# Convolution mixer of a four-layer trunk: TensorE's order written by hand, last shifted inputs copied between partitions, other priorities

## The chip, the cores and the metric

The kernel runs on one core of a Trainium2 chip. Five engines work side by side, each through its own list of instructions in order: TensorE (matmul, with its weight loads), VectorE (DVE), ScalarE (ACT), GpSimd (POOL) and SyncE (SP), whose queue issues the DMA copies. TensorE has a clock with two levels, 2.4 GHz and 1.2 GHz; the profile shows the level that was granted as a share of the full one. The metric is the device time of one execution in microseconds (us); less is better.

## The reference

A trunk of four layers over 512 tokens of 1024 channels, batch 1, float32. Each layer has a token mixer and a gated feed-forward block; each is framed by a modulation from a conditioning vector and a layer norm. The mixer of layer 0 is the one that the change touches:

```python
def conformer_conv_module(h, w_pw1, b_pw1, dw_w, dw_b, ln_g, ln_b, w_pw2, b_pw2):
    u = jax.nn.glu(h @ w_pw1 + b_pw1, axis=-1)          # 1024 -> 2 x 1024, a * sigmoid(g)
    u = causal_dwconv(u, dw_w, dw_b)                    # 31 taps along the tokens, per channel
    u = jax.nn.silu(layer_norm(u, ln_g, ln_b))          # norm over the 1024 channels
    return u @ w_pw2 + b_pw2

# around each mixer and each feed-forward block f
h = x * (1.0 + scale) + shift                           # shift, scale, gate: silu(c) @ ada_w + ada_b
x = layer_norm(DN_ALPHA * x + (1.0 + gate) * f(h), post_ln_g, post_ln_b)
```

## The kernel before

**Arithmetic.** A matrix product in float32 is made of three products of a cheaper type: weights and activations are each split into a high and a low part (hi and lo), and hi x hi, hi x lo and lo x hi are summed in PSUM. One block of weights (128 x 1024) is a unit: a 512 KB load by SP into `raw` (r_...), a ScalarE copy (wh_..., L282) and a VectorE subtraction (wl_..., L284), in units of the gated second projections preceded by a product with the gate row (L272). For the first projection a unit of 128 output channels is then 24 matmuls (L312).

**Layer 0's mixer** (`conformer`) runs over j = 0 to 7, blocks of 128 channels. Each takes two units of the first projection, one for the value (pa) and one for the gate (pg). ScalarE makes the sigmoid sg (L703), VectorE multiplies (L706) into `upad`, which has 30 zeros in front. The 31 taps are shared: the first three are VectorE operations on `upad` (L724, L726), the other 28 are matmuls. For these, R holds the input four times, shifted by 0 to 3 tokens and regrouped so that 32 channels x 4 shifts fill the 128 partitions: `upad` is written to DRAM (ud, L709) and read back by four copies (L711). lw (L714) are the diagonal weights. The convolution of block j (c0 to c7 in the text, `pc` in the trace, L720) is 28 matmuls, each shown as two. VectorE adds the two parts (cv, L728), TensorE transposes the sum to token-major form (ct, L692), ScalarE copies it (tm, L694), VectorE takes the statistics (L696). R and lw have two buffers each; the first projection has four PSUM banks, pc two, and the transposes and the gate's products share two (tr).

**Beside it** run the ada units: 48 per layer, each a load of 512 KB and a VectorE reduction (L238). `fill` adds one behind each unit of the projection (16 in this stage); `flush` brings those of a range that are still missing. Units 16 to 23 give the mixer's gate, 24 to 39 the modulation of the feed-forward block that follows. The gate is spread to a row by eight dg pieces (L472), two products on TensorE (gb, L475) and two ScalarE copies (L476).

**The end of the mixer.** For each 128 tokens t, `rstd` (L648 to L651, the power on POOL) and `normalise` (one half on VectorE, L660, one on ScalarE, L663) make the norm. For each half s of the tokens (two t's) and each j, TensorE transposes back (cb, L745), ScalarE applies silu (cs, L747), and ScalarE and VectorE split the result (cuh, cul). The second projection (p_pw with wh_pw first, L381) has eight units, whose 192 matmuls begin with the first three units on the first half of the tokens. Its results are added to X (L624), normalised and turned to the next h (hl, hh), with which the feed-forward block starts (p_f).

**What sets the order.** The program is traced in the order of the code; a scheduler then lists each engine's instructions by a simulated time and by priority, which is the place in the code unless `high_priority(offset)` moves it ahead by that many places (weights: 150). Where `manual_schedule` names an engine, that engine keeps the order of the code. The order of each list is fixed at compile time; at run time each engine takes its list in order and waits on semaphores.

Of the kernel before, what the change touches and what calls it, by code (L numbers as in the profile page):

```python
# [160 lines left out]
class Trunk:  # L161
# [504 lines left out]
    def conformer(self, nxt):  # L666
# [9 lines left out]
        with self.pool(name="cf", bufs=1, reuse_waits="tile") as op, ExitStack() as es, \  # L676
# [21 lines left out]
            self.apool, self.abufs = cf, CB  # L698
            for j in range(KD):
                pa = self.up(ins["pw1"], j, "pw1", fills=1)  # L700
                pg = self.up(ins["pw1"], KD + j, "pw1", fills=1)
                sg = self.sp.tile([P, T], F32, tag="u", bufs=4, name=f"sg{j}")
                nc.scalar.activation(out=sg, in_=pg, func=AF.Sigmoid, bias=bp1(KD + j))  # L703
                u = cf.tile([P, 544], F32, tag="upad", bufs=2, name=f"upad{j}")
                nc.vector.memset(u[:, :pad], 0.0)
                nc.vector.scalar_tensor_tensor(out=u[:, pad:pad + T], in0=pa, scalar=bp1(j), in1=sg, op0=ALU.add, op1=ALU.mult)  # L706
                R = cf.tile([P, 4, 544], F32, tag="R", bufs=2, name=f"R{j}")
                ud = dr.tile([P, 544], F32, tag="ud", bufs=2, name=f"ud{j}")
                nc.sync.dma_start(out=ud[:, nd:pad + T], in_=u[:, nd:pad + T])  # L709
                for q in range(4):  # L710
                    nc.sync.dma_start(out=R[32 * q:32 * q + 32, :, nd:pad + T - q],  # L711
                                      in_=ud[:, nd + q:pad + T].rearrange("(b c) x -> c b x", c=32))
                lw = cf.tile([P, CONV_G * 4, 32], F32, tag="lw", bufs=2, name=f"lw{j}")
                nc.vector.tensor_tensor(out=lw, in0=m4.rearrange("p (a c) -> p a c", a=1).broadcast_to([P, CONV_G * 4, 32]),  # L714
                                        in1=wpe[:, j, :].rearrange("p (a c) -> p a c", c=1).broadcast_to([P, CONV_G * 4, 32]),
                                        op=ALU.mult)
                pc = self.bank(f"pc{j}", "pc")
# [5 lines left out]
                o = cv[j]  # L723
                nc.vector.tensor_scalar(out=o, in0=u[:, :T], scalar1=dww(0, j), scalar2=dwb(j), op0=ALU.mult, op1=ALU.add)  # L724
                for tap in range(1, nd):
                    nc.vector.scalar_tensor_tensor(out=o, in0=u[:, tap:tap + T], scalar=dww(tap, j), in1=o,  # L726
                                                   op0=ALU.mult, op1=ALU.add)
                nc.vector.tensor_tensor(out=o, in0=pc, in1=o, op=ALU.add)  # L728
                token_major(j)
            self.flush(i, 24)  # L730
            self.apool = None
            gate = self.gate_rows(op, i, 0)
            es.close()
# [3 lines left out]
            for s in range(2):  # L737
                for t in (2 * s, 2 * s + 1):
                    mv = self.rstd(st[t], f"cf{t}")
                    self.normalise(tm[:, t, :], tm[:, t, :], mv)  # L740
                hs = slice(2 * s * P, 2 * (s + 1) * P)
# [686 lines left out]
```

## Time and profile before

| | us |
|---|---|
| median of 3 runs | 2688.15 |
| lowest and highest | 2685.92, 2689.37 |
| profiled execution | 2686.62 |
| its span, first to last instruction | 2684.8 |
| TensorE busy | 2603.4 |
| VectorE busy | 1992.3 |
| ScalarE busy | 1193.2 |

The profile is of one execution. Its times count from the first instruction; 1.82 us of the execution lie outside the span. The mixer of layer 0 takes about the first 240 us. A busy time of TensorE is the sum of matmul records, which overlap while they stream: a row of many matmuls that starts every 0.23 us is TensorE at its peak. The text in brackets behind a row of the timeline is the idle time of the engine just before it and what ended it.

### The profile page before, as it was taken

The numbers are of one execution on the slowest core, as the hardware profiler recorded it, in microseconds if no ns is written. First come the engines' busy times: TensorE is split into PE (matmuls) and PEld (weight loads), VectorE is DVE, ScalarE is ACT, GpSimd is POOL, SyncE is SP. The second block draws the span as 40 slices with busy tenths as digits, with TensorE's granted clock in tenths as the row PEclk, the third lists the DMA queues.
The fourth block names the chain that finished last, engine by engine and source line by source line (L and its number), as shares of the span: only waits on it lengthen the run. The fifth ranks groups of instructions, "written<-read, shape, count | busy, mean of one in ns | idle before, by whom it ended". The sixth has DMA issues, their size and how long they took to land.

```text
span 2684.8 us, 33858 instructions
## 1 busy us (share of the span) xinstructions
PE 2603.4 (97%) x13044; PEld 2095.9 (78%) x13044; DVE 1992.3 (74%) x3068; ACT 1193.2 (44%) x1758; POOL 43.8 (2%) x80
## 2 busy tenths in 40 slices
PE   8989999999997999999999999999999999999998
PEld 6548888887876788888887778888887777888886
DVE  7579997775778799677766777998676576766676
ACT  3134433345874543434545544543434454543432
POOL 0000000000000000000000000000000000000000
PEclk9989999999998999999999999999999999999999
DMA  8754864233221486222322223774323211323222
GB/s 320 211 170 162 302 231 142 98 102 102 85 66 45 155 303 204 98 97 95 100 81 71 95 81 108 244 256 158 100 97 94 94 56 48 102 98 115 94 96 77
DMA packets 109529, 352.66 MB, mean 131 GB/s; under 512 B 12088, under 2 KB 22328, under 8 KB 109368
## 3 DMA queue, kind: packets, MB, share of 16 engines
q1 hardware_dynamic: 109368, 350.50, 39.3%
q8 instruction: 102, 1.67, 0.3%
q14 instruction: 59, 0.48, 0.1%
HBM read 341.96 MB, written 8.50 MB: 131 GB/s over the span
## 4 chain that ended last, share of the span: by engine, by line
PE 83%; DVE 8%; ACT 5%; DMA 2%; issue 2%; POOL 1%; SPq 0%; POOLq 0%; DVEq 0%; ACTq 0%
PE p_f L312 35%; PE p_d L381 16%; PE p_mup L312 6%; PE p_mdn L381 3%; PE p_pw L312 3%; PE p_hqf L312 2%; PE p_sqk L312 2%; PE pc L720 1%; PE p_hv L381 1%; PE p_sv L381 1%; PE p_hg L312 1%; PE ms L1029 1%; ACT hf L545 1%; PE tr L540 1%; PE mn L1168 1%
## 5 line engine op out<-in xcount | busy, mean ns | idle before, releaser
L312 PE MATMUL p_f<-hl,wh_f 128*128 128x512 f32 (+1 forms) x1504 | 565.3, 376 | 1.9 <-DVE hl L552 1.9
L312 PE MATMUL p_f<-hh,wl_f 128*128 128x512 f32 (+1 forms) x1504 | 564.8, 376 | 0.0
L312 PE MATMUL p_f<-hh,wh_f 128*128 128x512 f32 (+1 forms) x1504 | 564.0, 376 | 0.1
L282 ACT CAST wh_f<-r_f 128x1024 fp32r<-128x1024 f32 x176 | 185.1, 1053 | 337.8 <-PE p_f L312 309.6
L312 PEld LDWEIGHTS p_f<-hl,wh_f 128*128 128x128 f32 x1504 | 283.1, 188 | 53.7 <-DVE hl L552 2.5
L312 PEld LDWEIGHTS p_f<-hh,wh_f 128*128 128x128 f32 x1504 | 282.5, 188 | 52.6 <-ACT hh L551 1.4
L312 PEld LDWEIGHTS p_f<-hh,wl_f 128*128 128x128 f32 x1504 | 283.1, 188 | 51.2 <-issue 0.2
L284 DVE TENSOR_TENSOR wl_f<-r_f,wh_f 128x1024 fp32r<-128x1024 f32 x176 | 215.2, 1224 | 134.3 <-ACT wh_f L282 133.8
L238 DVE CUSTOM_DVE_ANT_0 ada<-ada,sbc,adab 128x1024 f32<-128x1024 f32 x192 | 244.0, 1281 | 3.4 <-DMA ada<-in_ada_dram 3.4
L1359 DVE SCALAR_TENSOR_TENSOR cv<-p_f,par,cv 128x511 f32<-128x511 f32 (+1 forms) x176 | 131.5, 747 | 1.4
L1359 DVE SCALAR_TENSOR_TENSOR cg<-p_f,par,cg 128x511 f32<-128x511 f32 (+1 forms) x176 | 131.5, 747 | 1.3
L272 DVE TENSOR_TENSOR r_d<-r_d,gate 128x1024 f32<-128x1024 f32 x88 | 107.5, 1222 | 30.4 <-DMA r_d<-in_fdn_dram 29.9
L1369 ACT ACTIVATE cg<-cg 128x512 f32<-128x512 f32 x88 | 55.3, 629 | 159.3 <-DVE cg L1359 159.3
L284 DVE TENSOR_TENSOR wl_d<-r_d,wh_d 128x1024 fp32r<-128x1024 f32 x88 | 107.5, 1221 | 9.8 <-ACT wh_d L282 9.7
L312 PE MATMUL p_mup<-hh,wh_mup 128*128 128x512 f32 (+1 forms) x280 | 107.3, 383 | 0.9 <-ACT hf L545 0.9
L312 PE MATMUL p_mup<-hh,wl_mup 128*128 128x512 f32 (+1 forms) x280 | 106.1, 379 | 0.0
L312 PE MATMUL p_mup<-hl,wh_mup 128*128 128x512 f32 (+1 forms) x280 | 105.5, 377 | 0.0
L282 ACT CAST wh_d<-r_d 128x1024 fp32r<-128x1024 f32 x88 | 92.2, 1048 | 19.9 <-PE p_f L312 15.6
L663 ACT ACTIVATE X<-X,mv 128x512 f32<-128x512 f32 x56 | 43.1, 810 | 78.0 <-DVE mv L651 78.0
L1357 ACT ACTIVATE cg<-p_f,par 128x512 f32<-128x512 f32 x88 | 68.1, 774 | 13.9 <-PE p_f L312 13.9
L381 PE MATMUL p_d<-wl_d,gr2h 128*128 128x512 f32 x176 | 68.8, 391 | 0.0
L381 PE MATMUL p_d<-wl_d,gr0h 128*128 128x512 f32 x176 | 68.8, 391 | 0.0
(473 smaller groups left out, 5614.6 us busy)
## 6 DMA issues: line engine op xcount, KB each, us to landing
ada<-in_ada_dram SPq DMA_DIRECT2D x192, 512.0 KB, 4.6
r_f<-in_fup_dram SPq DMA_DIRECT2D x176, 512.0 KB, 4.0
r_d<-in_fdn_dram SPq DMA_DIRECT2D x88, 512.0 KB, 3.3
r_mup<-in_mup_dram SPq DMA_DIRECT2D x32, 512.0 KB, 3.3
r_pw<-in_pw_dram SPq DMA_DIRECT2D x24, 512.0 KB, 7.5
r_hqf<-in_hqf_dram SPq DMA_DIRECT2D x16, 512.0 KB, 3.3
r_mdn<-in_mdn_dram SPq DMA_DIRECT2D x16, 512.0 KB, 3.3
r_sqk<-in_sqk_dram SPq DMA_DIRECT2D x16, 512.0 KB, 3.5
```

Of the source, the lines that this page charges most:

```text
L238: nc.vector.tensor_tensor_reduce(out=raw, in0=raw, in1=self.sbc, scale=1.0, scalar=ab[:, j:j + 1], op0=ALU.mult, op1=ALU.add, accum_out=ac ...
L272: nc.vector.tensor_tensor(out=r, in0=r, in1=gr, op=ALU.mult)
L282: nc.scalar.copy(hi, raw)
L284: nc.vector.tensor_tensor(out=lo, in0=raw, in1=hi.bitcast(F32), op=ALU.subtract)
L312: self.nc.tensor.matmul(ps[:, c0:c1], a, b[:, k, c0:c1], start=(n == 0), stop=(n == 3 * KD - 1))
L381: self.nc.tensor.matmul(bank, l[:, ts_], r, start=(kp == first and a == n == 0), stop=(kp == last and a == 1 and n == 2))
L540: nc.tensor.transpose(ps[:, j * P:(j + 1) * P], n[:, k * P:(k + 1) * P], self.ident)
L545: nc.scalar.activation(out=hf[:, j, :], in_=ps[:, j * P:(j + 1) * P], func=AF.Identity, scale=G[:, k:k + 1], bias=B[:, k:k + 1])
L663: nc.scalar.activation(out=o[:, hs], in_=x[:, hs], func=AF.Identity, scale=mv[:, 2:3], bias=mv[:, 3:4])
L1357: nc.scalar.activation(out=o, in_=ps, func=AF.Identity, scale=w[2], bias=par[:, C_CONVB + m:C_CONVB + m + 1])
L1359: nc.vector.scalar_tensor_tensor(out=o[:, s:], in0=ps[:, :T - s], scalar=w[2 - s], in1=o[:, s:], op0=ALU.mult, op1=ALU.add)
L1369: nc.scalar.activation(out=cg, in_=cg, func=AF.Silu)
```

## The change

The change stays inside `conformer`. (1) The loop over j is cut into pieces, `unit`, `gating`, `convolve`, `back` and `gates`, which are put into one list, sorted by a number, and traced under `manual_schedule` for TensorE. The order that results on TensorE is: units 0 to 6, c0, u7, ct0, c1, u8, ct1, c2, u9, ct2, u10, c3, u11, ct3, u12, c4, u13, ct4, u14, c5, u15, ct5, the two gate products, c6, ct6, c7, ct7 (u: unit of the first projection, value and gate of a block in turn). (2) For the last block, j = 7, the write to DRAM and the four copies back are replaced by sixteen copies straight from `upad` to R, 32 partitions each. (3) Gating and lw get a priority of 200, the sum with its transposes, copy and statistics 400, and `rstd` and `normalise` 400. (4) Only units 0 to 12 bring an ada fill. (5) Behind the eighth sigmoid the table of silu is loaded ahead.

```diff
+            def unit(n):
+                j, z = divmod(n, 2)
+                px[n] = self.up(ins["pw1"], z * KD + j, "pw1", fills=int(n < 13))
+                if z:
+                    with tc.high_priority(offset=SPRIO):
+                        gating(j)
+            def gating(j):
                 sg = self.sp.tile([P, T], F32, tag="u", bufs=4, name=f"sg{j}")
+                act = nc.scalar.activation(out=sg, in_=px[2 * j + 1], func=AF.Sigmoid, bias=bp1(KD + j))
+                if j == KD - 1:
+                    with tc.issue_after(act.ins):
+                        nc.scalar.preload_act_table_set("silu_and_others")
...
+                if j == KD - 1:
+                    for q in range(4):
+                        for b in range(4):
+                            nc.sync.dma_start(out=R[32 * q:32 * q + 32, b, nd:pad + T - q], in_=u[32 * b:32 * b + 32, nd + q:pad + T])
+                else:
+                    ud = dr.tile([P, 544], F32, tag="ud", bufs=2, name=f"ud{j}")
...
+            def convolve(j):
+                R = us["R", j]
+                with tc.high_priority(offset=SPRIO):
+                    lw = cf.tile([P, CONV_G * 4, 32], F32, tag="lw", bufs=2, name=f"lw{j}")
...
+            def back(j):
+                with tc.high_priority(offset=2 * SPRIO):
+                    nc.vector.tensor_tensor(out=cv[j], in0=pcs[j], in1=cv[j], op=ALU.add)
+                    token_major(j)
+
+            def gates():
+                self.flush(i, 24)
+                us["gate"] = self.gate_rows(op, i, 0)
+
+            todo = [(n, lambda n=n: unit(n)) for n in range(2 * KD)] + [(2 * KD - 0.5, gates)]
+            for j in range(KD):
+                todo.append((min(max(2 * j + 4.5, j + 6.5), 2 * KD + 0.2 * (j - KD)), lambda j=j: convolve(j)))
+                todo.append((min(max(2 * j + 5.6, j + 7.4), 2 * KD + 0.2 * (j - KD) + (0.1 if j > 5 else -0.05)), lambda j=j: back(j)))
+            todo.sort(key=lambda x: x[0])
+            with tc.manual_schedule(engines={mybir.EngineType.PE}):
+                for _, fn in todo:
+                    fn()
...
                 for t in (2 * s, 2 * s + 1):
-                    mv = self.rstd(st[t], f"cf{t}")
-                    self.normalise(tm[:, t, :], tm[:, t, :], mv)
+                    with tc.high_priority(offset=2 * SPRIO):
+                        mv = self.rstd(st[t], f"cf{t}")
+                        self.normalise(tm[:, t, :], tm[:, t, :], mv)
```

## Rows read from the trace of the kernel before

**Rows 1.** The page, part 1: busy us (share of the span) and instructions of each engine.

```profile
PE 2603.4 (97%) x13044; PEld 2095.9 (78%) x13044; DVE 1992.3 (74%) x3068; ACT 1193.2 (44%) x1758; POOL 43.8 (2%) x80
```

**Rows 2.** Table of stretches: length, then busy us (instructions) by engine, granted clock, DMA share, GB/s.

```profile
155.80:175.90 20.10, 16.31 (x124) 4.71 (x122) 11.04 (x20) 3.85 (x5) 0.00 (x0) 0.92 0.41 102
175.90:189.10 13.20, 5.12 (x18) 2.45 (x15) 9.78 (x26) 6.29 (x10) 3.31 (x4) 0.62 0.80 287
189.10:200.20 11.10, 11.10 (x55) 8.74 (x54) 10.51 (x28) 9.58 (x21) 0.00 (x0) 0.84 0.49 162
200.20:221.00 20.80, 20.80 (x93) 17.22 (x92) 20.45 (x27) 7.36 (x9) 0.00 (x0) 1.00 0.44 142
```

**Rows 3.** Timeline, TensorE's matmuls: start us, us, engine, line, what, times [idle before <-releaser].

```profile
49.09 0.50 PE L312 MATMUL p_pw<-hh_first,wh_pw 128*128 128x512 f32 x1
49.43 0.40 PE L312 MATMUL p_pw<-hl_first,wh_pw 128*128 128x512 f32 x1
49.66 0.40 PE L312 MATMUL p_pw<-hh_first,wl_pw 128*128 128x512 f32 x1
...
95.85 0.66 PE L692 MATMUL ct<-ident,cv 128*128 128x128 f32 x4 [0.81 <-DVE cv L728]
...
158.01 0.72 PE L692 MATMUL ct<-ident,cv 128*128 128x128 f32 x4 [2.20 <-DVE cv L728]
...
167.38 0.63 PE L692 MATMUL ct<-ident,cv 128*128 128x128 f32 x4 [0.92 <-DVE cv L728]
...
169.73 6.22 PE L720 MATMUL pc<-R,lw 128*32 128x512 f32 x56
...
180.47 1.12 PE L692 MATMUL ct<-ident,cv 128*128 128x128 f32 x4 [4.52 <-DVE cv L728]
...
182.26 2.07 PE L475 MATMUL gb<-dg,onesr 128*128 128x512 f32 x2 [0.67 <-ACT tm L694]
...
185.60 1.09 PE L745 MATMUL cb<-ident,tm 128*128 128x128 f32 x4 [1.26 <-DVE tm L660]
...
189.10 1.20 PE L381 MATMUL p_pw<-wh_pw,cuh 128*128 128x512 f32 x2
...
240.81 0.39 PE L312 MATMUL p_f<-hl,wh_f 128*128 128x256 f32 x1 [0.72 <-DVE hl L552]
```

**Rows 4.** Timeline of VectorE, the same columns.

```profile
49.08 1.61 DVE L706 SCALAR_TENSOR_TENSOR upad<-p_pw,cpar,sg 128x512 f32<-128x512 f32 x2 [0.32 <-ACT sg L703]
...
153.65 1.28 DVE L238 CUSTOM_DVE_ANT_0 ada<-ada,sbc,adab 128x1024 f32<-128x1024 f32 x1
...
170.46 2.36 DVE L272 TENSOR_TENSOR r_pw<-r_pw,gate 128x1024 f32<-128x1024 f32 x2 [0.93 <-ACT gate L476]
...
179.73 0.69 DVE L728 TENSOR_TENSOR cv<-pc,cv 128x512 f32<-128x512 f32 x1
...
187.77 1.22 DVE L272 TENSOR_TENSOR r_pw<-r_pw,gate 128x1024 f32<-128x1024 f32 x1
```

**Rows 5.** The chain of waits in order of time: start us, us, what.

```profile
158.73 7.78 PE pc L720 x56
...
208.51 1.22 DVE wl_pw L284
```

**Rows 6.** Timeline of SP's queue: issue start us, us, what, number of copies.

```profile
58.33 2.83 SPq L711 DMA_DIRECT2D R<-ud  x4
...
155.87 1.75 SPq L711 DMA_DIRECT2D R<-ud  x4
```

**Rows 7.** DMA issues of 140 to 185 us: queue, number, KB, median us to landing.

```profile
ud<-upad SPq DMA_DIRECT2D x1, 269.5 KB, 2.5
...
R<-ud SPq DMA_DIRECT2D x1, 268.0 KB, 6.0
```

**Rows 8.** Timeline of ScalarE, columns as in rows 3.

```profile
186.39 1.28 ACT L747 ACT_TABLE_LOAD   x1
...
187.69 0.56 ACT L747 ACTIVATE cs<-cb,cpar 128x256 f32<-128x256 f32 x1
```

More of the change, by code (lines that the diff above doesn't have):

```diff
@@ new lines, in conformer @@
+            us, pcs, px = {}, {}, {}
+            def unit(n):
[5 more added lines that the diff above has]
+            def gating(j):
+                sg = self.sp.tile([P, T], F32, tag="u", bufs=4, name=f"sg{j}")
+                act = nc.scalar.activation(out=sg, in_=px[2 * j + 1], func=AF.Sigmoid, bias=bp1(KD + j))
+                if j == KD - 1:
+                    with tc.issue_after(act.ins):
+                        nc.scalar.preload_act_table_set("silu_and_others")
+                u = us[j] = cf.tile([P, 544], F32, tag="upad", bufs=2, name=f"upad{j}")
+                nc.vector.memset(u[:, :pad], 0.0)
+                nc.vector.scalar_tensor_tensor(out=u[:, pad:pad + T], in0=px[2 * j], scalar=bp1(j), in1=sg, op0=ALU.add, op1=ALU.mult)
+                R = us["R", j] = cf.tile([P, 4, 544], F32, tag="R", bufs=2, name=f"R{j}")
+                if j == KD - 1:
[4 more added lines that the diff above has]
+                    ud = dr.tile([P, 544], F32, tag="ud", bufs=2, name=f"ud{j}")
+                    nc.sync.dma_start(out=ud[:, nd:pad + T], in_=u[:, nd:pad + T])
+                    for q in range(4):
+                        nc.sync.dma_start(out=R[32 * q:32 * q + 32, :, nd:pad + T - q],
+                                          in_=ud[:, nd + q:pad + T].rearrange("(b c) x -> c b x", c=32))
+                o = cv[j]
+                nc.vector.tensor_scalar(out=o, in0=u[:, :T], scalar1=dww(0, j), scalar2=dwb(j), op0=ALU.mult, op1=ALU.add)
+                for tap in range(1, nd):
+                    nc.vector.scalar_tensor_tensor(out=o, in0=u[:, tap:tap + T], scalar=dww(tap, j), in1=o,
+                                                   op0=ALU.mult, op1=ALU.add)
@@ new lines, in convolve @@
+            def convolve(j):
+                R = us["R", j]
+                with tc.high_priority(offset=SPRIO):
+                    lw = cf.tile([P, CONV_G * 4, 32], F32, tag="lw", bufs=2, name=f"lw{j}")
+                    nc.vector.tensor_tensor(out=lw, in0=m4.rearrange("p (a c) -> p a c", a=1).broadcast_to([P, CONV_G * 4, 32]),
+                                            in1=wpe[:, j, :].rearrange("p (a c) -> p a c", c=1).broadcast_to([P, CONV_G * 4, 32]),
+                                            op=ALU.mult)
+                pc = pcs[j] = self.bank(f"pc{j}", "pc")
@@ L722, in conformer @@
                                          tile_position=(0, 32 * cb))
[L723 to L730, printed above, removed]
+            def back(j):
[13 more added lines that the diff above has]
+                    fn()
             self.apool = None
-            gate = self.gate_rows(op, i, 0)
+            gate = us["gate"]
             es.close()
```

17 lines of the change are left out of this document (removed).

## Prediction

> **What bounds the kernel now.** I read the page first: TensorE is busy 97% of the span [rows 1], so whatever the change gives must come from a stretch where TensorE stands still or runs at half clock. The table of stretches of the convolution mixer, read next, shows where that is: while units and convolutions mix, TensorE is full; from 155.8 to 175.9 us it is busy 16.3 of 20.1 us, and from 175.9 to 189.1 us only 5.1 of 13.2 us, at a granted clock of 0.62 on the mean, between the half level (1.2 GHz) and the full one (2.4 GHz) [rows 2]. Third the timeline of TensorE there: it waits 2.20 us for the sum cv5, 0.9 us for cv6, 4.52 us for cv7 and 1.26 us for the first normalised tile, and starts the second projection (p_pw with wh_pw, L381) at 189.10 [rows 3]. Fourth the timeline of VectorE: those sums are late since it works in order and other work stands ahead of them, three ada reductions in front of cv5, and weights of the second projection (L272, L284) in front of cv7 [rows 4]. Last the chain of waits: through the second projection it runs over VectorE (from 208.5 us on) and comes back to TensorE at the start of the feed-forward block, which waits 0.72 us for hl before 240.81 [rows 3, 5]. VectorE is busy 10.5 of 11.1 and 20.5 of 20.8 us there [rows 2]. So two limits lie close together: TensorE up to 189 us, VectorE just behind it after.
>
> Call E the moment at which all sixteen units, c0 to c5 (the convolutions) and ct0 to ct4 (their transposes) are done. Before, E is 158.01 - 2.20 = 155.81 us and the second projection starts 33.3 us later. Except for the 3.8 us of ada work below, the engines' total work is unchanged; what changes is the order.
>
> **The change, part by part.**
>
> *Order by hand up to E.* The sum of TensorE's work is the same; c5 moves ahead of the last unit, which alone gains nothing. Two known waits change. The wait of ct1 at 95.85 (0.81 us) goes, because a unit now stands between c1 and ct1: -0.8. Unit 4 now comes strictly before unit 5 and takes the PSUM bank that the first upad operation reads until about 49.08 + 0.75 = 49.83 us, where TensorE before started another unit at 49.09 [rows 3, 4]: +0.7. New is that c0 stands behind unit 6 and holds back everything after it until R0 has landed. It is due at 49.83 + 3 units x 24 matmuls x 0.23 us = 66.4 us [rows 3]. R0 was issued from 58.33 to 61.2 us [rows 6] and the slowest of these copies in the late stretch landed 6.0 us after its issue [rows 7]: 67.2 us. So 0 to 0.8 us; I take 0, since the new priority puts upad's copy ahead of the ada loads. E stays at 155.7 us.
>
> *From E to c7.* Now ct5 (0.4 us), two gate products (2.07 us for one at half clock [rows 3], so 1.0 to 1.1 each), c6, ct6, c7. The second gate product needs ct5's bank back (a ScalarE copy, behind the last sigmoid and perhaps the table load) and four dg pieces on VectorE behind upad7 and three taps: c6 starts between E + 2.6 (no wait) and E + 5.7; I take 4.3. c6 lasts 6.2 us; the sum, now first in VectorE's queue, and ct6 take 0.74 us to ct's start [rows 3, 4] and some 0.9 more for drain and ct: c7 could start at E + 12.1.
>
> *R7 directly.* A write to DRAM (landing in 2.5 us) and four copies go; sixteen small copies come. All sixteen are issued by SP one after another: four took 1.75 us [rows 6], so 0.44 us each and 7.0 us in all, where one write and four copies cost 2.2 us of issue. Sigmoid and upad end about E + 1.6, the last issue begins at E + 8.3, and landing takes 2.5 (the write alone) to 6.0 us (the last of four big copies) [rows 7]: R7 is there at E + 10.8 to 14.3. I take 3.5 us, nearer to the short end as each copy is a quarter as large: E + 11.8, just hidden behind ct6. Queued behind the sixteen on SP are only loads of the second projection, needed 15 us later.
>
> *Sums and norm first.* c7 ends at E + 12.1 + 6.2 = E + 18.3. ct7 follows 0.85 us later instead of 4.52 us: -3.7. From ct7 to the first cb transpose it took 185.60 - 180.47 = 5.13 us [rows 3]; ct7 itself, at full clock again, is 0.5 us shorter: 4.6.
>
> *Silu's table ahead.* The load stood between the normalising pieces and the first silu: 1.28 us, then the silu at 187.69, 1.30 after the load's start [rows 8]. It moves to ScalarE's idle time around E. But the pieces of the second half of the tokens now have priority too and can take its place: two pieces of about 0.76 us. From the first cb to the projection it took 3.5 us [rows 3]; bounds 2.2 (the table alone) and 3.8 (1.5 in, 1.3 out); I take 3.5, a gain of zero. The Trainium skill (ScalarE: Activation LUTs, What ACT_TABLE_LOAD costs) gives a drain of 1.38 us on top of a load of 1.28 us; no such drain stands in this trace, where the silu starts 0.02 us after the load. By the page this step would be worth 1.4 us more.
>
> So the projection starts at E + 18.3 + 0.85 + 4.6 + 3.5 = E + 27.25 = 182.95 us, against 189.10: **-6.1 us**.
>
> *Clock.* After the 2.2 us wait before ct5, c6 took 7.78 us where c7, at 2.4 GHz, took 6.22 [rows 3, 5]: 1.6 us lost to a clock that fell to its half level behind the wait. The new waits between E and c6 sum to 0 to 3 us, so such a dip costs 0 to 1.6 us; I take half, **+0.8**. The half-clock stretch around the norm (0.62 from 175.9 to 189.1, 0.84 to 200.2 [rows 2]) comes after a similar idle time and stays.
>
> *Ada units moved.* Three of the convolution stage's sixteen fills go (13 remain), so eleven instead of eight ada units are left for the stretch of the second projection: three loads of 512 KB, DMA share there is 0.44 to 0.49 [rows 2], hidden; and 3 x 1.28 = 3.84 us of VectorE [rows 4], which have to be done before the modulation of the next block. Between 189.1 and 221 us VectorE has 0.9 us free [rows 2], and the chain runs over it: up to +2.9. In its 3.4 idle us of 175.9 to 189.1 they would cost nothing. I take **+1.4**, the middle.
>
> The sum is -6.1 + 0.8 + 1.4 = **-3.9 us**. The profiled execution took 2686.62 us (span 2684.8 plus 1.82) and gives 2682.7; the median of the runs is 1.53 us above it, so 2684.2. Behind the mixer TensorE streams, so the shift is carried to the end one for one.
>
> **The rivals.**
>
> *All covered.* c6 starts without a wait, R7 lands at E + 10.8, no dip, the ada units fit ahead of the projection: -6.1 - 1.3 = -7.4 us, 2680.7; with the table's 1.3 us as well 2679.4. For it: VectorE idles 9 of the 20.1 us from 155.8 [rows 2]. Against: the projection's VectorE is full.
>
> *R7 is the new wait.* Its last copy needs 6.0 us: c7 starts at E + 14.3, +2.2 us, 2686.4. For it: SP issues in order, each copy at 0.44 us; against: the copies are small and DRAM is left out.
>
> *Weights become late (slower).* Before, nine operations on the second projection's weights (six of L272, three of L284; the first at 170.46, the last at 187.77 [rows 4]) are done ahead of the projection, in part at the cost of cv7. Behind sums and norm they fall into the stretch where VectorE is full: 9 x 1.18 = 10.6 us, with the ada units 14.4, less 0.9 free: -6.1 + 0.8 + 13.5 = +8.2 us, 2696.4. It is slower than before as soon as three of the nine are displaced and all ada units cost. Against it: between the first gate row and c7's end VectorE has some 15 us, of which taps, dg and sums fill about 7.
>
> *Copies in a row (slower).* If a copy's fixed time did not overlap with the next, sixteen would take 16 x 2.5 us = 40 us by the shortest landing [rows 7], c7 would start 30 us later: 2714. Against: four R copies were issued in 1.75 us and the last landed 6.0 us after issue. The Trainium skill (DMA: Bandwidth & Descriptors, Anatomy of one DMA) counts about 2 us for each DMA plus its bytes and advises large batches; by that, 16 x 2.15 us is an estimate of 34 us.
>
> *It does not do what it says.* Only TensorE's order is fixed; the other engines' stays with the scheduler, which could put ada ahead of the sums again: about no change, 2688.
>
> **How the numbers follow.** Forecast 2684.2: 0.48, its own range 2681.5 to 2687. All covered 0.24; R7 0.14; weights late 0.08; copies in a row 0.02; nothing 0.04. The range goes from 2679.4 (all covered with the table) to 2689.7: -6.1 + 2.2 (R7) + 1.6 (dip) + 2.9 (ada) + 0.8 (R0) = +1.4. About 0.2% or 5.4 us is what a measurement of this kernel can tell from no change. Faster by more than that is under 2682.8: all covered and a quarter of the forecast, 0.36. Slower is over 2693.5: the two slower rivals and a remainder, 0.11. The same: 0.53.
>
> **What would show it.** c5 ahead of the last unit and E near 155.7; no wait of ct7 above 1 us; c7 starting at E + 11 to 13 with ct6 or R as its releaser; table load right behind the eighth sigmoid; the first p_pw of L381 near 183; eleven ada reductions after it and VectorE without gaps up to the next block. Wrong would make it: a wait at c0 or c2 over 1 us, c7 released by the copies at E + 14 or later, weights' operations of L272 behind L660, or a p_f start that has not moved with p_pw.

## The result, and the profile after

| | before | after |
|---|---|---|
| median of 4 runs, us | 2688.70 | 2708.76 |
| lowest and highest | 2685.92, 2689.37 | 2706.58, 2713.56 |
| profiled execution, its span | 2686.62, 2684.8 | 2713.56, 2711.8 |

The ratio is 1.0076 with a 95% interval of 1.0064 to 1.0088: the change makes the kernel 20 us slower, where 4 us faster were predicted and the range ended at 2689.7. The profiled execution is the slowest of the four; some 7 us of its excess arise behind the mixer, where both kernels have the same instructions, so the argument below ends at the start of the feed-forward block (the first matmul p_f of L312). There the two traces differ by 259.55 - 239.46 = 20.1 us.

The page alone doesn't find them. TensorE's busy time grew by 15.3 us against [rows 1] although it does the same work (6.2 of them up to the first p_f): a matmul at a low clock counts as busy for longer, and the granted clock is 0.984 over the whole span instead of 0.990.

```profile
PE 2618.7 (97%) x13044; PEld 2106.6 (78%) x13044; DVE 1991.2 (73%) x3068; ACT 1193.5 (44%) x1758; POOL 43.6 (2%) x80
```

Three stretches of the mixer hold the loss. The table of stretches of the changed kernel (length, then busy us and instructions of PE, PEld, DVE, ACT and POOL, granted clock, DMA share, GB/s):

```profile
100.00:120.00 20.00, 12.48 (x49) 9.02 (x42) 13.42 (x23) 3.15 (x4) 0.00 (x0) 0.77 0.54 155
...
170.50:192.10 21.60, 16.99 (x125) 4.70 (x123) 10.26 (x21) 6.30 (x8) 0.00 (x0) 0.92 0.42 125
192.10:200.32 8.22, 2.51 (x12) 1.65 (x13) 7.30 (x21) 4.53 (x8) 2.47 (x3) 0.75 0.99 358
200.32:259.55 59.23, 53.01 (x239) 42.26 (x237) 56.16 (x109) 27.99 (x48) 2.77 (x6) 0.93 0.54 190
```

The kernel before, in the first and the last of these stretches:

```profile
100.00:120.00 20.00, 20.00 (x135) 11.34 (x128) 8.61 (x16) 2.69 (x3) 0.00 (x0) 1.00 0.79 239
...
189.10:239.46 50.36, 50.27 (x234) 40.92 (x232) 47.17 (x89) 26.25 (x47) 1.10 (x2) 0.97 0.39 128
```

The first row of the changed kernel shows a new loss: in the middle of the units, where TensorE was full before (20.00 of 20.00 us), it now stands still for 7.5 us and has a granted clock of 0.77. The next two are the tail that the prediction was about. The last runs from the first matmul p_pw of the second projection to the first p_f, and takes 59.2 us where it took 50.4.

The timeline of TensorE in the changed kernel (start us, us, engine, line, what, times, [idle before <-releaser]):

```profile
37.67 0.66 PE L579 MATMUL tr_first<-ident,X 128*128 128x128 f32 x4 [2.10 <-ACT hf_first L581]
...
49.86 1.19 PE L312 MATMUL p_pw<-hh_first,wh_pw 128*128 128x512 f32 x4 [0.59 <-ACT hh_first L582]
53.53 0.50 PE L312 MATMUL p_pw<-hh_first,wh_pw 128*128 128x512 f32 x1 [0.66 <-DVE upad L717]
...
108.69 0.50 PE L312 MATMUL p_pw<-hh_first,wh_pw 128*128 128x512 f32 x1 [1.76 <-ACT wh_pw L282]
...
115.18 0.80 PE L312 MATMUL p_pw<-hh_first,wl_pw 128*128 128x512 f32 x1 [5.75 <-DVE wl_pw L284]
115.78 0.63 PE L312 MATMUL p_pw<-hh_first,wh_pw 128*128 128x512 f32 x1
116.20 0.63 PE L312 MATMUL p_pw<-hl_first,wh_pw 128*128 128x512 f32 x1
...
170.80 1.02 PE L475 MATMUL gb<-dg,onesr 128*128 128x512 f32 x2
175.52 1.82 PE L475 MATMUL gb<-dg,onesr 128*128 128x512 f32 x2 [3.69 <-DVE dg L472]
177.27 7.14 PE L745 MATMUL pc<-R,lw 128*32 128x512 f32 x56
185.32 0.63 PE L692 MATMUL ct<-ident,cv 128*128 128x128 f32 x4 [0.92 <-DVE cv L751]
185.88 6.22 PE L745 MATMUL pc<-R,lw 128*32 128x512 f32 x56
193.00 0.63 PE L692 MATMUL ct<-ident,cv 128*128 128x128 f32 x4 [0.91 <-DVE cv L751]
198.00 1.09 PE L782 MATMUL cb<-ident,tm 128*128 128x128 f32 x4 [4.37 <-DVE tm L660]
...
200.32 1.20 PE L381 MATMUL p_pw<-wh_pw,cuh 128*128 128x512 f32 x2
...
240.76 0.50 PE L381 MATMUL p_pw<-wh_pw,cuh 128*128 128x512 f32 x1 [1.16 <-DVE X L624]
...
255.83 1.37 PE L540 MATMUL tr<-ident,X 128*128 128x128 f32 x8 [2.99 <-ACT X L663]
...
258.79 1.11 PE L540 MATMUL tr<-ident,X 128*128 128x128 f32 x4 [1.59 <-ACT X L663]
```

What the reader is to see there:

- **Head.** The last matmuls on the first hidden tile (the row at 49.86) started at 46.14 us before: they are 3.7 us late before any unit of the new order has begun. Unit 4 (53.53) then waits 0.66 us for its bank, which was predicted: it is 4.4 us later than in [rows 3].
- **Unit 10.** It waits 1.76 us for its wh and 5.75 us for its wl, and its other 22 matmuls take 8.07 us instead of 22 x 0.24 = 5.3 us, since from 115.78 to 120.90 us they start 0.43 us apart: 10.3 us lost. The last unit ends at 170.53 instead of the 155.7 predicted for E.
- **Tail.** From E to the first p_pw it takes 200.32 - 170.53 = 29.8 us, 3.5 less than before; 27.25 were predicted.
- **Second projection.** It waits for X, which VectorE and ScalarE deliver late, from 240 us on: the stretch is 8.9 us longer than before, and of these only the 1.4 for ada units were predicted.

Why unit 10's weight is late stands in the lists of the other engines. ScalarE, VectorE and SP in the changed kernel:

```profile
106.53 0.69 ACT L711 ACTIVATE sg<-p_pw,cpar 128x512 f32<-128x512 f32 x1 [11.24 <-PE p_pw L312]
107.12 0.58 ACT L694 COPY tm<-ct 128x512 f32<-128x512 f32 x1
107.58 1.06 ACT L282 CAST wh_pw<-r_pw 128x1024 fp32r<-128x1024 f32 x1
...
107.73 0.88 DVE L696 BATCH_NORM_STATS2 cst<-tm 128x6 f32<-128x128 f32 x4 [3.95 <-ACT tm L694]
...
112.03 1.28 DVE L238 CUSTOM_DVE_ANT_0 ada<-ada,sbc,adab 128x1024 f32<-128x1024 f32 x1
...
113.24 0.75 DVE L732 SCALAR_TENSOR_TENSOR cv<-upad,cpar,cv 128x512 f32<-128x512 f32 x1
113.90 1.22 DVE L284 TENSOR_TENSOR wl_pw<-r_pw,wh_pw 128x1024 fp32r<-128x1024 f32 x1
...
83.51 0.32 SPq L725 DMA_DIRECT2D ud<-upad  x1
83.94 6.66 SPq L727 DMA_DIRECT2D R<-ud  x8
90.65 2.14 SPq L237 DMA_DIRECT2D ada<-in_ada_dram  x4
93.45 0.33 SPq L267 DMA_DIRECT2D r_pw<-in_pw_dram  x1
```

The weight's load is issued at 93.45 us, behind a copy of upad that SP waited for, eight copies of R and four ada loads. It landed 9.3 us later, near 102.8 us, still in time for unit 10, which could have begun at 106.9. But its cast to wh stands in ScalarE's list behind the sigmoid sg4, which needs unit 9: ScalarE idles for 11.24 us, with the cast behind the waiting sigmoid. VectorE's list had itself stood still until 107.73 us, for the copy tm behind that sigmoid; in it wl comes after the statistics, upad, two taps and three ada reductions. In the order written by hand nothing may take unit 10's place on TensorE.

### The profile page after: what moved, and what is told of

It reads as the page before. It is cut to its first block, busy times and chain, and to the rows that moved or that the text cites. A ratio compares the mean times of both kernels' runs of the same rounds, so it can differ in the third digit from the quotient of the medians.

```text
span 2711.8 us, 33879 instructions
## 1 busy us (share of the span) xinstructions
PE 2618.7 (97%) x13044; PEld 2106.6 (78%) x13044; DVE 1991.2 (73%) x3068; ACT 1193.5 (44%) x1758; POOL 43.6 (2%) x80
## 4 chain that ended last, share of the span: by engine, by line
PE 82%; DVE 8%; ACT 4%; issue 2%; DMA 2%; POOL 1%; SPq 0%; POOLq 0%; DVEq 0%; ACTq 0%
PE p_f L312 35%; PE p_d L381 16%; PE p_mup L312 6%; PE p_mdn L381 3%; PE p_pw L312 3%; PE p_hqf L312 2%; PE p_sqk L312 2%; PE pc L745 2%; PE p_hv L381 1%; PE p_sv L381 1%; PE ms L1066 1%; PE p_pw L381 1%; ACT hf L545 1%; PE tr L540 1%; PE p_hg L312 1%
## 5 line engine op out<-in xcount | busy, mean ns | idle before, releaser
L312 PE MATMUL p_f<-hl,wh_f 128*128 128x512 f32 (+1 forms) x1504 | 566.2, 377 | 1.2 <-DVE hl L552 1.2
L312 PE MATMUL p_f<-hh,wl_f 128*128 128x512 f32 (+1 forms) x1504 | 565.4, 376 | 0.0
L312 PE MATMUL p_f<-hh,wh_f 128*128 128x512 f32 (+1 forms) x1504 | 565.2, 377 | 0.0
L312 PEld LDWEIGHTS p_f<-hl,wh_f 128*128 128x128 f32 x1504 | 283.9, 189 | 52.8 <-DVE hl L552 1.6
L312 PEld LDWEIGHTS p_f<-hh,wl_f 128*128 128x128 f32 x1504 | 283.8, 189 | 51.6 <-issue 0.2
L312 PEld LDWEIGHTS p_f<-hh,wh_f 128*128 128x128 f32 x1504 | 283.6, 189 | 51.7 <-ACT hh L551 0.9
L272 DVE TENSOR_TENSOR r_d<-r_d,gate 128x1024 f32<-128x1024 f32 x88 | 107.5, 1222 | 36.4 <-DMA r_d<-in_fdn_dram 35.9
L312 PE MATMUL p_mup<-hh,wh_mup 128*128 128x512 f32 (+1 forms) x280 | 108.6, 388 | 0.9 <-ACT hf L545 0.9
L312 PE MATMUL p_mup<-hh,wl_mup 128*128 128x512 f32 (+1 forms) x280 | 107.7, 385 | 0.0
L312 PE MATMUL p_mup<-hl,wh_mup 128*128 128x512 f32 (+1 forms) x280 | 106.7, 381 | 0.0
L1394 ACT ACTIVATE cv<-p_f,par 128x512 f32<-128x512 f32 x88 | 68.1, 774 | 3.9 <-PE p_f L312 3.9
```

Of the source, the lines that this page charges most:

```text
L272: nc.vector.tensor_tensor(out=r, in0=r, in1=gr, op=ALU.mult)
L312: self.nc.tensor.matmul(ps[:, c0:c1], a, b[:, k, c0:c1], start=(n == 0), stop=(n == 3 * KD - 1))
L1394: nc.scalar.activation(out=o, in_=ps, func=AF.Identity, scale=w[2], bias=par[:, C_CONVB + m:C_CONVB + m + 1])
```

## The experiments

Theory A: the priorities and the place of the pieces in the code push weights back in the in-order lists of SP, ScalarE and VectorE. Rival B: TensorE's strict order is itself the cause, whatever stands on the other engines. The table has the times of the profiled executions, read from TensorE's timelines; "E" is the end of the last of units and c0 to c5. The edits are shown shortened, with values in place of the names of constants.

| run | unit 4 | E | first p_pw | first p_f | ratio to before, 95% |
|---|---|---|---|---|---|
| before | 49.09 | 155.81 | 189.10 | 239.46 | |
| after | 53.53 | 170.53 | 200.32 | 259.55 | 1.0076 (1.0064 to 1.0088) |
| e1 order alone | 54.56 | 160.72 | 192.53 | 245.30 | 1.0022 (1.0012 to 1.0031) |
| e2 gating without priority | 54.64 | 160.79 | 191.41 | 244.73 | 1.0023 (1.0013 to 1.0032) |
| e3 head | 50.31 | 170.74 | 201.02 | 255.96 | 1.0066 (1.0051 to 1.0081) |
| e4 scheduler's order | | 163.67 | 192.60 | 247.33 | 1.0027 (1.0016 to 1.0038) |
| e5 = e2 and e3 | 50.49 | 160.53 | 191.37 | 246.26 | 1.0017 (1.0008 to 1.0026) |
| e6 = e5, 16 fills | 50.22 | 157.64 | 187.03 | 241.20 | 1.0009 (1.0000 to 1.0018) |
| e7 = e6, 24 fills | 50.03 | 163.83 | 199.23 | 251.29 | 1.0040 (1.0028 to 1.0053) |
| e8 = e6 without the tail's steps | 50.52 | 158.30 | 189.76 | 243.13 | 1.0016 (1.0007 to 1.0025) |
| e9 = e6, last unit ahead of c5 | 50.74 | 157.54 | 183.29 | 233.91 | 0.9980 (0.9971 to 0.9989) |
| e10 = e9, R7 directly | 50.30 | 157.09 | 179.18 | 235.16 | 0.9980 (0.9971 to 0.9989) |
| e11 = before, sums and norm first | | 159.89 | 193.90 | 245.76 | 1.0011 (1.0002 to 1.0020) |
| e12 = e10, 22 fills | 50.75 | | 185.48 | 237.89 | 0.9991 (0.9982 to 1.0000) |

Single profiles differ by some 2 us behind 600 us, so a difference below that is read from the ratio alone.

**e1, TensorE's order by hand alone.** Against the changed kernel:

```diff
-                px[n] = self.up(..., fills=int(n < 13))
+                px[n] = self.up(..., fills=1)
-                    with tc.high_priority(offset=SPRIO):       # gating, taps' weights
+                    with tc.high_priority(offset=0):
-                    with tc.high_priority(offset=2 * SPRIO):   # sums, norm
+                    with tc.high_priority(offset=0):
-                if j == KD - 1:                                # silu's table, R7 directly
+                if False:
```

> Only TensorE's order by hand: no priority on gating, taps' weights, sums or norm, 16 fills, R7 through DRAM, no silu table ahead. Theory A (the priorities push the weights back in the in-order queues of SP, ScalarE and VectorE): the 3.7 us ahead of the first unit and the 0.7 us of unit 4's bank stay, since both come from the place of the pieces in the code; the stall at unit 10 (1.76 + 5.75 us of wait and the half-clock stretch behind it) is gone; the wait of some 4.5 us ahead of ct7 is back. That is 2688.7 + 4.4 = 2693, at most 2697. Rival B (a strict order on TensorE itself exposes waits and clock falls, whatever has priority elsewhere): the 10 us stay, 2703 or more.

Measured: 2695.83 us against 2689.97 of before. Unit 4 is at 54.56 us, the wait of ct7 is back (4.26 us), unit 10 doesn't wait. The strict order alone costs nothing between unit 4 and E: 160.72 - 54.56 = 106.2 us, against 106.7 before. Its 5.9 us are the 5.5 by which unit 4 starts late. B as stated falls. The loss at the head is there without any of the priorities; e4 shows whether it needs the strict order.

**e2, gating and the taps' weights without priority.**

```diff
-                    with tc.high_priority(offset=SPRIO):       # gating, taps' weights
+                    with tc.high_priority(offset=0):
```

> The change with the priority of 200 taken from gating and the taps' weights alone. Theory A: the load of unit 10's weight is issued ahead of ud3 and R2 again, no wait over 1 us at units 10 and 11, TensorE busy over 17.5 of the 20 us from 100 to 120 us: 10.3 us back, 2708.8 - 10.3 = 2698.5, give or take 3. Rival B: the waits at units 10 and 11 stay or come at another place of the strict order, 2706 to 2710.

Measured: 2696.07 us; 14 of the 20 us come back. The same stretch as in the first row of the table of the changed kernel, in this run:

```profile
100.00:120.00 20.00, 20.00 (x130) 11.78 (x123) 10.26 (x18) 3.18 (x4) 0.00 (x0) 1.00 0.41 110
```

And unit 10's cast in its timeline of ScalarE:

```profile
84.16 1.06 ACT L290 CAST wh_pw<-r_pw 128x1024 fp32r<-128x1024 f32 x1
```

TensorE is full at full clock, and the cast that ran at 107.58 us in the changed kernel runs at 84.16. So the priority of 200 on gating and the taps' weights is a cause of the stall at unit 10; the two were not taken away one by one. At the first p_f the two traces differ by 14.8 us: 9.7 of them come back by E and 5.9 in the stretch of the second projection, ahead of which all nine of the weights' operations run again (table below); 0.8 are lost between the two.

**e3, the head.** The weights of the first ten units get 60 instead of 150.

```diff
-        with self.tc.high_priority(offset=prio):               # prio=WPRIO in every unit
+        with self.tc.high_priority(offset=prio):               # prio=60 in units 0 to 9 of the mixer
```

> The change with the priority of the weights of the first ten units lowered from 150 to 60, so that their loads no longer stand ahead of the ada loads of the stage before. Theory A: first_h (k = 7) ends near 46.1 us again instead of 49.9, no wait of hf_first over 2 us for adac: 3.7 us back, 2705; no change at unit 10. If the 3.7 us were hidden by the later stall at unit 10 (which waits for a load that does not depend on them): 2708.8, with a longer wait at unit 10. Rival B: 2708.8, as TensorE's order is the same.

Measured: 2707.78 us, no difference that can be told from the changed kernel. The head is repaired (unit 4 at 50.31), and the gain is gone at unit 10, in TensorE's timeline of this run:

```profile
112.35 0.79 PE L322 MATMUL p_pw<-hh_first,wh_pw 128*128 128x512 f32 x1 [8.63 <-ACT wh_pw L292]
...
129.98 0.50 PE L322 MATMUL p_pw<-hh_first,wl_pw 128*128 128x512 f32 x1 [2.28 <-DVE wl_pw L294]
```

The waits sum to 10.9 us instead of 7.5: what comes earlier waits longer (the second wait is that of unit 11), and E is again 170.7. Of the three outcomes written down, the second holds. A repair ahead of a fixed later stall shows nothing by E. In this one profile the stretch of the second projection is 4.3 us shorter than in the changed kernel, with the weights' operations ahead of it again; the times of all runs neither show nor exclude such a gain.

**e4, the order left to the scheduler.** All priorities as in the change.

```diff
-            with tc.manual_schedule(engines={mybir.EngineType.PE}):
+            with ExitStack():
```

> The change with TensorE's order left to the scheduler, all priorities as in the change. Rival B: without the strict order the scheduler puts other work into the holes, 2692 or less. Theory A: the weights still come late by the order of SP, ScalarE and VectorE, so at most a third of the 20 us comes back: 2702 to 2712.

Measured: 2697.37 us, better than A allows and worse than B wants. The head is as late as in the change (the last matmuls on the first hidden tile start at 50.58 us), without the strict order here and without the priorities in e1: it belongs to the place of the pieces in the code. The stretch around unit 10 shows why:

```profile
100.00:120.00 20.00, 17.76 (x140) 6.27 (x140) 15.54 (x29) 4.88 (x6) 0.00 (x0) 1.00 0.93 302
```

While the weight of unit 10 is late, the scheduler's order runs c2, c3 and a part of c4 (their inputs were there), so TensorE is busy 17.8 of 20 us and the clock stays at 1.00. In the change the strict order keeps these same convolutions behind unit 10. The stall thus needs both: weights that the priority made late (A) and an order that lets nothing pass (B). Undoing either brings back 13 to 14 us of the 20.

**e5, both repairs together**, the edits of e2 and e3.

> The change with both repairs: weights of the first ten units at priority 60, gating and the taps' weights without one. If the head (3.7 to 4.8 us ahead of unit 4) and the stall at unit 10 are two separate losses in a row, of which the later one absorbs the gain of the earlier as long as it stands: E, the end of the last unit, near 156 us, and the time of run e2 less 4.7 us, 1.4 us over before (2691.4 with before at 2690). If the head's repair is worth nothing at all: as e2, 6 us over before.

Measured: 2692.48 us against 2689.23. By the ratio this is 2.2 to 7.0 us over before: not the 1.4 that was expected, and no difference from e2 that can be told. E is 160.5 and not 156. Unit 4 starts 4.2 us earlier than in e2, and c0 gives it back:

```profile
69.24 1.49 PE L755 MATMUL pc<-R,lw 128*32 128x512 f32 x8 [2.11 <-DMA R<-ud]
```

It waits 2.11 us for R0, and c0 takes 7.91 instead of 6.22 us at the clock that fell behind the wait. So the priority of gating had a use for the first chunk: in the change, and in e3 with the head repaired, c0 followed unit 6 without a wait.

**e6, sixteen fills**, the edits of e5 and:

```diff
-                px[n] = self.up(..., fills=int(n < 13))
+                px[n] = self.up(..., fills=1)
```

> As the run with both repairs, and all sixteen units of the mixer fill again, so that eight ada reductions and not eleven are left for the second projection. If VectorE sets the end of that stretch, all of 3 x 1.28 = 3.8 us comes back: 2.4 us under before (2687.6 with before at 2690). If the three are hidden by half, as predicted: 1.4 us back, level with before. If hidden: no change to the run without them.

Measured: 2691.40 us, 1 to 2 us under e5 (by medians and by ratios), with intervals that overlap. The size of the ada term isn't settled by this pair: with the three ada reductions gone, two more products of a weight with the gate row fell behind the first p_pw (table of VectorE's time below), so that the stretch became only 0.7 us shorter.

**e7, 24 fills**: eight units of the mixer fill twice.

```diff
-                px[n] = self.up(..., fills=1)
+                px[n] = self.up(..., fills=1 + n % 2)
```

> As the run with both repairs and 16 fills, and eight units of the mixer fill twice, so that no ada reduction is left for the second projection: 8 x 1.28 = 10.2 us of VectorE's work go from that stretch to the one from 60 to 160 us, where VectorE is idle for a third of the time. If VectorE sets the end of the second projection: 3 to 6 us under the run with 16 fills (TensorE's own work is then the limit), 2682 to 2685 with before at 2690. If TensorE or the weights' loads set it: no change. If the added loads (4 MB) or reductions make the mixer's weights late: slower by 3 us or more, with waits at units 8 to 12.

Measured: 2697.93 us, the third outcome in size, with the waits at c0 and c7 and not at units 8 to 12. On SP an added ada load stands ahead of the first chunk's copy to DRAM (issued at 58.07 us, in e6 at 51.89), loads stand between R7's copies (the last of them issued at 181.1 us), and TensorE waits for both:

```profile
71.64 8.81 PE L755 MATMUL pc<-R,lw 128*32 128x512 f32 x56 [4.99 <-DMA R<-ud]
...
181.50 1.52 PE L755 MATMUL pc<-R,lw 128*32 128x512 f32 x3 [5.68 <-DMA R<-upad]
```

**e8, without the steps of the tail**, the edits of e6 and, against them, no priority for sums and norm, R7 through DRAM, silu's table where it was.

> As the run with both repairs and 16 fills, but without the four steps of the tail: no priority for sums and norm, R7 through DRAM, silu's table left where it was. What the tail's steps are worth as predicted: 5.3 us (the 6.1 less the clock's 0.8), so 5 us slower than the run with 16 fills. If what they give at the start of the second projection is lost ahead of the feed-forward block, since the weights' operations and loads that stood there move behind: within 1.5 us of the run with 16 fills.

Measured: 2693.48 us, 2.1 us above e6. The tail's steps are worth some 2 us (the intervals overlap), not the 5.3 predicted. From E to the first p_pw e8 takes 189.76 - 158.30 = 31.5 us, against 29.4 us in e6; from there to the first p_f e6 loses 0.8 of it. One part of it is silu's table: the second pair of cb waits for the first silu 1.33 us here and 0.44 us in e6 and in the changed kernel.

**e9, the last unit ahead of c5.** From e6: R7 through DRAM, a third R tile (R7 no longer waits for c5 to release R5's), gating of the first two chunks at 200 again, and another order of the tail:

```diff
-   ... u14, c5, u15, ct5, both gate products, c6, ct6, c7, ct7
+   ... u14, u15, gate product 0, c5, c6, gate product 1, ct5, c7, ct6, ct7
```

> As the run with both repairs and 16 fills (e6), with three further edits: the last unit stands ahead of c5 and not behind it (with a third R tile, R7 through DRAM again), the two gate products stand apart (one ahead of c5, one behind c6) and ct5 to ct7 move behind the convolution that follows them; gating of the first two chunks keeps the priority of 200, so that R0 lands before c0. Theory: in e6 c7 starts 13.6 us after E, since R7, the gate's dg pieces and ct6 follow the last unit; with c5 and c6 to cover them, ct7 starts about 6.5 us earlier (near 173 and not 179.7 us), c0 waits under 0.5 us. If the second projection is then set by TensorE: 5 to 7 us under e6, 2684 to 2686 with before at 2689. If VectorE sets the start of the feed-forward block (near 240 us in every run so far): at most 1.5 us under e6, with waits of TensorE for X around 222 to 241 us.

Measured: 2683.88 us against 2688.77, faster than before by 0.2% (0.1 to 0.3%), the first outcome at its lower end. c0 doesn't wait, c5 and c6 run without a break at full clock, and nothing of the tail waits until ct7:

```profile
175.48 0.63 PE L705 MATMUL ct<-ident,cv 128*128 128x128 f32 x4 [3.69 <-DVE cv L764]
```

ct7 starts at 175.48 us, where 173 was expected. This wait is the very one that the change was to remove, with the priority of 400 on the sum. VectorE's timeline in e9 says why it is back:

```profile
170.06 1.22 DVE L285 TENSOR_TENSOR r_pw<-r_pw,gate 128x1024 f32<-128x1024 f32 x1
173.51 1.23 DVE L285 TENSOR_TENSOR r_pw<-r_pw,gate 128x1024 f32<-128x1024 f32 x1 [2.23 <-DMA r_pw<-in_pw_dram]
174.65 0.68 DVE L764 TENSOR_TENSOR cv<-pc,cv 128x512 f32<-128x512 f32 x1
```

The list has a weight's operation ahead of the sum, and that operation waits for its load. c7 ended at 171.2, so the sum was ready and stood in line for 3.4 us.

**e10, the same with R7 by sixteen copies.**

> As e9, with R7 from partition to partition by sixteen copies. In e6 the sixteen took 10.7 us of issue on SP (0.67 each, not the 0.44 predicted), and the second projection's weights are queued behind them. Theory: R7 is there about 1.6 + 10.7 + 2.5 = 14.8 us after the last unit, so c7 waits some 1 to 3 us for it, against none through DRAM (1.6 + 0.4 + 2.5 + 1.8 + 6.0 = 12.3 us): 1 to 3 us slower than e9. Rival: the direct way is the faster one, as it saves the DRAM write: level or up to 2 us faster.

Measured: 2683.09 us, level with e9, which is the rival's outcome; c7 doesn't wait for R7, as the theory had it. SP's queue:

```profile
151.62 10.64 SPq L735 DMA_DIRECT2D R<-upad  x16
162.36 1.51 SPq L280 DMA_DIRECT2D r_pw<-in_pw_dram  x3
```

Sixteen issues take 10.64 us, and the loads of the second projection start 10 us later than in e9 (152.45). The sum of cv7 runs here behind four of the weights' operations and not nine as in e9, since the others weren't loaded yet: ct7 waits 0.82 us, the projection starts at 179.18, 9.9 us earlier than before and 4.1 earlier than in e9. The feed-forward block starts 1.2 us later than in e9 all the same, after waits for X:

```profile
230.56 0.66 PE L553 MATMUL tr<-ident,X 128*128 128x128 f32 x4 [0.89 <-ACT X L676]
...
232.30 1.12 PE L553 MATMUL tr<-ident,X 128*128 128x128 f32 x4 [1.08 <-ACT X L676]
...
234.40 1.11 PE L553 MATMUL tr<-ident,X 128*128 128x128 f32 x4 [0.98 <-ACT X L676]
```

**e11, sums and norm first on the kernel before.**

```diff
-                nc.vector.tensor_tensor(out=o, in0=pc, in1=o, op=ALU.add)
-                token_major(j)
+                with tc.high_priority(offset=400):
+                    nc.vector.tensor_tensor(out=o, in0=pc, in1=o, op=ALU.add)
+                    token_major(j)
-                    mv = self.rstd(st[t], f"cf{t}")
-                    self.normalise(tm[:, t, :], tm[:, t, :], mv)
+                    with tc.high_priority(offset=400):
+                        mv = self.rstd(st[t], f"cf{t}")
+                        self.normalise(tm[:, t, :], tm[:, t, :], mv)
```

> The kernel before with one part of the change: priority 400 for the sums, their transposes and the norm; nothing else. As predicted: the wait of ct7 falls from 4.5 to 0.9 us, the projection starts 3.7 us or more earlier and the time falls by as much, 2685 with before at 2689. Theory now: the wait of ct7 goes, but weights' operations that were done ahead of the projection move into it, where VectorE is full, so the feed-forward block starts at most 1.5 us earlier: 2687.5 to 2690.

Measured: 2691.72 us, 3 us slower than before (0.5 to 5), which neither line expected. The wait that was to go is there, 4.42 us against 4.52, and the same seven operations on weights run ahead of the sum:

```profile
184.37 1.11 PE L692 MATMUL ct<-ident,cv 128*128 128x128 f32 x4 [4.42 <-DVE cv L729]
```

The priority alone doesn't put the sum first: the scheduler fills VectorE's idle time ahead of the sum with what is ready by its own estimate, and an in-order engine then runs the list as it stands. E comes 4 us later: c0 starts 2.0 us later without a wait of TensorE, and a transpose at 125.35 us waits 1.74 us for its sum; the rest and the reason for either weren't followed further.

**e12, six more fills on e10**: units 5, 7, 9, 11, 13 and 15 fill twice, two ada reductions are left for the second projection.

> As e10, and units 5, 7, 9, 11, 13 and 15 fill twice, so that two ada reductions and not eight are left for the second projection. In e10 the projection starts 9.9 us earlier than before and the feed-forward block only 4.3 us earlier, with waits of TensorE for X from 230 us on. If VectorE's work between the two is what holds the block back: 6 x 1.28 = 7.7 us less of it there, the block starts near 231 us and the time is 3 to 5 us under e9 and e10 (2679 to 2681 with before at 2689). If the weights' loads, or the chain of norm and transposes for X, hold it: within 1 us of e10. If the added loads delay a unit or R7: slower than e10, with a wait of TensorE over 1 us ahead of 175 us.

Measured: 2685.92 us, about 3 us over e10 by the ratios, whose intervals overlap. The waits are those of the third outcome: R2 is 1.84 us late, the gate's dg pieces 3.05 us, and c5 and c6 take 13.60 instead of 12.24 us at the clock behind it. But the stretch from the first p_pw to the first p_f became 3.6 us shorter. That stretch, from the tables of stretches of these runs:

| run | length, us | TensorE busy | VectorE busy | ada in it | weights' operations in it |
|---|---|---|---|---|---|
| before | 50.36 | 50.27 | 47.17 | 8 | 7 |
| after | 59.23 | 53.01 | 56.16 | 11 | 9 |
| e2 | 53.32 | 50.56 | 51.27 | 11 | 7 |
| e3 | 54.94 | 52.02 | 51.40 | 11 | 7 |
| e5 | 54.89 | 51.52 | 51.47 | 11 | 7 |
| e6 | 54.17 | 50.60 | 51.71 | 8 | 9 |
| e8 | 53.37 | 52.61 | 48.99 | 8 | 7 |
| e9 | 50.62 | 50.62 | 47.97 | 8 | 7 |
| e10 | 55.98 | 52.59 | 53.58 | 8 | 10 |
| e12 | 52.41 | 51.36 | 45.76 | 2 | 10 |
| e7 | 52.06 | 51.01 | 38.51 | 0 | 7 |

The stretch is never shorter than TensorE's 50.3 us. In e8 the granted clock is 0.50 and 0.66 in its first 5 us and the next 5 (before: 0.65 and 1.00), and it is 3 us longer. Where VectorE has over 51 us to do, the stretch is 2 to 3.5 us longer than VectorE's work. Taking more away, as in e12 and e7, then gives nothing. So both engines limit it, and before they lay 3 us apart. Three more ada reductions alone go with 3.0 to 4.6 us more than before (e2, e3, e5), the later weights alone with 3.8 (e6), and both with 8.9 (after).

## Why the prediction was wrong, step by step

**E, the step that failed.** "The sum of TensorE's work is the same ... E stays at 155.7 us" took the order of the other engines for given. E came 14.7 us later: 3.7 at the head, 0.7 for unit 4's bank (predicted), 10.3 at unit 10, less the wait of ct1 (predicted, -0.8); 0.8 is not accounted for. Two pieces of the diff that had been read did it. Gating's priority of 200 moves sigmoid, upad, taps and copies of every chunk, not of the last alone, past the weights' 150 on ScalarE, VectorE and SP; the prediction counted what is queued behind a moved DMA only for R7. And with the convolutions' pieces later in the code, units come earlier in it, so that their loads pass the ada loads of the stage before: on SP three loads of weights (r_pw) now take the place from 17.58 us on where before six ada loads stood at 18.68, and the last three hf_first of ScalarE wait for adac 3.03, 0.99 and 3.23 us, before 0.98, 1.23 and 1.76. The first of these rows is from the changed kernel, the second from the kernel before:

```profile
17.58 9.27 SPq L267 DMA_DIRECT2D r_pw<-in_pw_dram  x3
...
18.68 7.76 SPq L237 DMA_DIRECT2D ada<-in_ada_dram  x6
```

**The rival "weights become late"** had the mechanism and 0.08, and the wrong weights. It was priced for those of the second projection alone. Displaced were first those of the units, and the point from which that decides is a stalled sigmoid ahead of a cast in ScalarE's list. That a strict order on TensorE turns a late weight into idle time, and e4's order hardly does, wasn't in any rival.

**From E to c7**: predicted were c6 at E + 4.3 (at most 5.7) and c7 at E + 12.1; they came at E + 6.7 and E + 15.35. dg waited 3.69 us, as VectorE had its pieces between the taps of the last chunk, and the gate product behind the wait took 1.82 us at the half clock instead of 1.02.

**R7** was hidden, as predicted, but by a longer way: sixteen issues took 10.6 to 10.7 us in the changed kernel, in e6 and in e10, 0.66 each and not the 0.44 of [rows 6], and a copy landed 2.0 to 2.8 us after its issue (medians of four copies each). "Copies in a row" is refuted, they overlap. The Trainium skill (DMA: Bandwidth & Descriptors, Anatomy of one DMA, written for DMAs issued from GpSimd) has some 50 ns of sequencer time in the fixed 2 us of a DMA. The landing agrees with these 2 us; the issue on SP's queue here, with 0.66 us, doesn't agree with the 50 ns, by which sixteen issues are an estimate of 0.8 us and not 10.6. That these loads are "needed 15 us later" was the miss: seven of the nine weights' operations still came ahead of the projection, two didn't.

**Sums first**: ct7 follows c7 after 0.91 us (0.85 predicted), the right size for an incomplete reason. e11 and e9 show that the priority doesn't bring it; in the change and in e10 the weights' loads sat behind the sixteen copies, and so fewer of their operations were there to be put ahead.

**Norm and table**: ct7 to the first cb 5.0 us (4.6 predicted), cb to the projection 2.3 (3.5 predicted, 2.2 the bound with the table's full gain). The load runs at 171.75 us behind the eighth sigmoid, and the 1.2 us are gained. The Trainium skill (ScalarE: Activation LUTs, What ACT_TABLE_LOAD costs) puts load and drain at 2.66 us together. By that, 2.7 us is an estimate of what was there to gain; the trace has no more than the load's own 1.28.

**The clock's dip** was right in kind, and its size in part by luck: c6 took 7.14 us, 0.9 more than c7 (0.8 predicted), but the wait before it was 3.69 us where 0 to 3 had been assumed, and the gate product between them took another 0.8 us of the low clock.

**From the projection on.** "The shift is carried to the end one for one" and the +1.4 for three ada units failed together: 8.9 us. VectorE has 56.16 us of work there instead of 47.17 [rows 2]: 3 ada reductions (3.8), 2 operations L272 (2.4), and 2.7 of pieces of X and the norm that now fall ahead of the first p_f. With the eleven ada reductions and the weights in their place the stretch is 3.0 to 4.6 us longer than before (e2, e3, e5): this puts the ada term at or above its upper bound of 2.9, not at 1.4. With eight ada reductions and the weights late it is 3.8 us longer (e6): the step "needed 15 us later" is the other part. The runs differ in other things too, so the shares are not shown to more than about 1 us. Each displaced piece was costed alone, while VectorE had 3 us to spare for all of them.

The sum at the first p_f: 14.7 - 3.5 + 8.9 = 20.1 us. (Two figures of the prediction miss their own terms by 0.1 us, the last issue for R7 and the end of the range; nothing hangs on it.) The tail, which the whole range was about, moved as forecast in sign and by 3.5 of the 6.1 us in size; a TensorE that was read as full hid that it was full only as long as every list beside it stayed in its order.

**A better version.** e9 and e10 are 0.2% faster than before: the priority kept where it has a use (the first two chunks), the units' loads back in their place, and c5 and c6 put where the last chunk's copies can hide.

## What to carry to other kernels

Before an order is written by hand for one engine, or a priority is given to a chain, list what the chain passes on each of the other in-order queues, for every iteration and not for the last alone: an instruction that waits at the head of ScalarE's list holds the weights' cast behind it. A strict order has to have its inputs early; fix the late ones first, and repair all stalls of a chain together, since a later one absorbs what the earlier ones give (e3, e5). A gain at the start of a stretch is worth only what its second engine has to spare (3 us here).

## What the runs showed of the hardware

An issue of a small copy from partition to partition costs SP's queue 0.66 us in a row of sixteen (10.6 to 10.7 us in the changed kernel, in e6 and in e10), half as much again as the 0.44 of four larger copies, and the queue's next loads start only then. The cost of a wait is more than the wait: 7.5 us without matmuls at unit 10 left TensorE at a granted clock of 0.77 over 20 us, and over the next 5.7 us its matmuls started 0.43 us apart and more instead of 0.24, another 2.8 us.
